# Moving the SBUF pools of a float32 decoder kernel from 64 and 192 bytes past a multiple of 256 onto the multiple itself

## The chip, the cores and the metric

The kernel runs on one core of a Trainium2 chip. The time is the device time of one execution in microseconds (us); the time before is 1786.8 us, the median of three runs (1786.62 to 1786.98). Five engines share the core: TensorE (PE, with its weight loads shown apart as PEld), VectorE (DVE), ScalarE (ACT), GpSimd (POOL) and SyncE (SP, which here only issues DMA). SBUF is the on-chip memory: 128 partitions, each a row of bytes; a tile is a range of bytes at one address in all partitions, and "address" below always means the byte offset in a partition.

## The reference: what is computed

Two residual layers on a sequence of 512 positions with 1024 channels, and a last RMSNorm. All is float32. Per layer:

```
h = rmsnorm(x, norm1_g);  p = h @ w_in                       # 1024 x 7424 columns
y_rw  = rwkv7_branch(...)      # token shift, decay, 8 heads of 64, recurrence over time
y_ret = retention_branch(...)  # rotary, 4 heads, chunks of 128
y_sg  = sgu_branch(...)        # gelu, layer norm, causal mixing in chunks of 128
x = x + sum_g(sigmoid(gate_g) * (y_g @ w_branch[g])) @ w_out
u = rmsnorm(x, norm2_g) @ ffn_w_up                           # 1024 x 5632
c = causal depthwise conv of width 3 over u
x = x + (silu(c[:, :2816]) * c[:, 2816:]) @ ffn_w_down       # 2816 x 1024
```

Nearly all arithmetic is in the products with the large weights.

## The kernel before

**Products in three passes.** A float32 product is made of float32r passes on TensorE. Each operand is split into a rounded part `hi` and a rest `lo` (ScalarE makes `hi` by a cast, VectorE subtracts to get `lo`), and `mm3` (L140) issues three matmuls into one accumulator: weight hi with activation lo, hi with hi, lo with hi. Each is its own pass: a weight load of 128 x 128 (the stationary operand) and a matmul that streams the moving operand, 128 partitions x 512 columns of 4 bytes, that is 2048 contiguous bytes of every partition. `matF` (L152) does this for the k-blocks of one output block of 128 channels. The program has 6,934 such passes with 512 columns and, in `finish` (L945), 132 with 256 columns.

**Weights.** `unit` (L89) gives the next 128 x 512 block of a weight: `load` (L112) issues its DMA from SP into one of three raw buffers `wr`, `part` (L120) makes the hi and lo. The parts lie in the pool `wp` (tiles `wh`, `wl`) in the first half of a layer, and later in the pools of `self.f`, `self.r` or `self.u` (tiles `sh`, `sl`). The order of the units is noted in a first build and replayed in the second with a look-ahead of 2 to 5 units (`AHEAD`, L26).

**Order.** Instructions of one engine run in the order that the tile framework's planner gives; places that must not be moved are pinned (`keep_in_program_order`). In the RWKV-7 part, products of the gates, retention and spatial gating are handed out as filler (`fillers`, L350) between the dependent steps: 33 steps of filler while `solve` (L632) inverts the chunk matrices on VectorE, then one step between the steps of the recurrence (L542 to L611).

**Where tiles lie.** The pools are laid one behind another in every partition, in the order in which they are opened (L55 to L59), and each tile takes its bytes rounded up to 32. A 16 KiB area for DMA and four constants of 32 bytes come first, so `cp` begins at 16,512. With the sizes of the code:

| pool | what it holds | address before | past a multiple of 256 |
|---|---|---|---|
| `cp` | `con` 3748 bytes, `rst` 2048, `bonesR` 512, `ones` 512 | 16,512 | `con` 128, the rest 64 |
| `wp` | `wr`, `wh`, `wl`: 3 tiles of 2048 each | 23,360 | 64 |
| `up` | 31 tiles of 2048 (`self.u`): normed `hi`/`lo`, gate and conv tiles, `x` | 41,792 | 64 |
| `rg` | 16 tiles of 2048 (`self.r`) | 105,280 | 64 |
| `sp` | small tiles: two buffers of each unless said otherwise; `rsF`, the row of norm factors, is one buffer of 528 columns of which 512 are used; `R` | 138,048 | mixed; `rsF` 64, `R` 192 |
| `rw0`, `rw1` (first half of a layer) | `GB`, `F`, `UB`, `ag`, `bk`, `cs`, ... | 145,856 | `GB` 192, `ag`, `bk`, `cs` 64 |
| `ff0`, `ff1` (the rest of the layer) | 39 tiles of 2048 (`self.f`) | 145,856 | 192 |

Tiles of 2048 bytes keep the remainder of their pool, and slices of weights start at multiples of 512 bytes inside a tile, so every operand of `mm3` starts at its pool's remainder.

**Which passes stream from which pool.** From `ff` (192 past): per layer the merges of three branches (L864: 24 x 4 k-blocks x 3 passes = 288), `wout` (L877: 8 x 8 x 3 = 192), the transposed spatial-gating product (L812: 4 x 8 x 3 = 96) and four triples in `rwkv_out` (12); and in `ffn_down` (L924) the tiles `ah`, of which 39 of 44 lie in `ff` (L896 to L898): 59 of 66 passes per output block, 15 blocks, 885. In all 2 x 588 + 885 = 2,061, and 118 of the 132 passes of 256 columns. The other 4,873 passes of 512 columns stream from `up`, `wp` or `rg` (64 past): all of `ffn_up` (L892), the RWKV columns, gates and retention projections.

The functions touched are `norm_rows` (L226, the buffer `rsF`), `run` (L258, the tile `ones`) and `rwkv` (L384, the tile `omu`, 1 minus the token-shift weight, read by `col` at L412).

Of the kernel before, what the change touches and what calls it, by code (L numbers as in the profile page):

```python
# [8 lines left out]
F32 = mybir.dt.float32  # L9
# [37 lines left out]
class Emit:  # L47
# [178 lines left out]
    def norm_rows(self):  # L226
        pb = self.sm()
        for c in range(NC):
            self.tc.keep_in_program_order(self.nc.tensor.transpose(pb[:, c * 128:c * 128 + 128], self.rsT[:, c:c + 1].to_broadcast([128, 128]), self.c("ident")))
        self.rsF = self.small((128, 528), "rsF", bufs=1)[:, :512]  # L230
        self.nc.scalar.copy(self.rsF, pb)

    def firstF(self, l, ids, st, at):
# [24 lines left out]
    def run(self):  # L258
        nc, tc, a, V = self.nc, self.tc, self.a, self.nc.vector
        self.con = self.cp.tile([128, NCC], F32, name="con")  # L260
        self.rst = self.cp.tile([128, 512], F32, name="rst")
        self.bonesR = self.cp.tile([128, 128], F32R, name="bonesR")
        self.ones = self.cp.tile([128, 128], F32, name="ones")
        V.memset(self.rst, 1.0)
        V.memset(self.ones, 1.0)
        nc.scalar.copy(self.small((128, 1), "ms"), self.rst[:, 0:1])
        wu = self.acc()
        for i in range(6):
            nc.tensor.matmul(wu[:, 0:256], self.rst[:, 0:128], self.rst[:, 256:512], start=True, stop=True)
        self.load_pc(0)  # L270
        st = self.norm_new()
        xs = [self.u(n="x") for _ in range(8)]
        self.keep = True
        with tc.high_priority():
            for j in range(8):
                tc.keep_in_program_order((nc.scalar if j in (1, 3) else nc.sync).dma_start(xs[j], a["xT"][:, j, :]))
                if self.plan and j in (0, 2, 3):
                    self.load(self.plan[self.nraw])
        for step in "z0 w z1 z2 w z3 w z4 z5 w z6 z7 w s0 s1 s2 w s3 s4 s5 s6 s7".split():
            if step == "w":  # L280
                if self.plan:
                    if self.nraw == self.npart:
                        self.load(self.plan[self.nraw])
                    self.part(self.plan[self.npart])
            elif step[0] == "z":
                self.norm_z(st, xs[int(step[1])], "n1")
            else:
                self.norm_sq(st, xs[int(step[1])])
        self.keep = False
        tc.keep_in_program_order(nc.scalar.dma_start(self.con, a["con"]))  # L290
        xd = [a["xT"][:, j, :] for j in range(8)]
        for l in range(L):
            mg = self.mixer(l, st)
            st = self.norm_new()
            x = self.wout(l, mg, xd, st)
            act = self.ffn_up(l, st)
            st = self.norm_new()
            x, xd = self.ffn_down(l, act, x, st)
            if l == L - 1:
                self.finish(l, act, x, st["acc"])  # L300
            self.rp.__exit__(None, None, None)
            self.fp = None
# [81 lines left out]
    def rwkv(self, l, nst):  # L384
# [1 line left out]
        T, P = nc.tensor, nc.gpsimd  # L386
        q8 = lambda t: t.rearrange("p (c t) -> p c t", t=64)
        pcol = lambda n, w: self.pc[:, PC[n]:PC[n] + w]
        omu = self.small((128, 14), "omu")
        V.tensor_scalar(omu, pcol("mu", 14), -1.0, 1.0, op0=MUL, op1=ADD)  # L390
        haw = self.small((128, 8), "haw")
        V.tensor_scalar(haw, pcol("a0", 8), 0.5, None, op0=MUL)
# [722 lines left out]
```

## Time and profile before

| | |
|---|---|
| time, median of 3 runs | 1786.8 us |
| the profiled execution | 1787.56 us, its span 1785.5 us |
| granted TensorE clock over the span | 0.997 |
| PE busy | 1770.2 us, 9,646 matmuls |
| VectorE busy | 1160.3 us |
| ScalarE busy | 784.7 us |
| GpSimd busy | 192.9 us |
| bytes moved by DMA | 193.27 MB, 108 GB/s over the span |
| the longest chain | PE 97% of the span, line 144 alone 88% |

The profile names instructions by line: all passes of `mm3` stand at L144, told apart by tile names, written `acc<-moving,stationary`. The mean duration of a matmul there is its time from first to last column through a pipeline; passes overlap, so that what a pass costs is the distance from its start to the next one's start. That is read from the timeline, which lists the start of every instruction.

### The profile page before, as it was taken

How to read it: one execution, taken by the hardware profiler on the slowest of the kernel's cores; microseconds unless marked ns; L12 is line 12 of the kernel's file. 1: busy time of each engine (PE TensorE's matmuls, PEld its weight loads, DVE VectorE, ACT ScalarE, POOL GpSimd, SP SyncE). 2: the span in 40 equal slices, each digit the busy share in tenths (PEclk: the TensorE clock that was granted, in tenths of full speed). 3: DMA queues.
4: the chain of work that ended last, by engine and by line, in shares of the span. 5: the costliest groups of instructions: out<-in, count | busy, mean ns of one | idle time of the engine just before them, and what ended most of it. 6: DMA issues, size and time to landing. Idle time of an engine off the chain costs nothing.

```text
span 1785.5 us, 25916 instructions
## 1 busy us (share of the span) xinstructions
PE 1770.2 (99%) x9646; PEld 1443.6 (81%) x9646; DVE 1160.3 (65%) x1996; ACT 784.7 (44%) x1333; POOL 192.9 (11%) x240
## 2 busy tenths in 40 slices
PE   9999999999999999999999999999999999999998
PEld 7878877888788888888887788778887888888887
DVE  6887736468667777753358875455676687777333
ACT  5564444544344444343245544445332454443321
POOL 0132012013300000000002220220132000000000
PEclk9999999999999999999999999999999999999999
DMA  5234432324543333243332343324144433332332
GB/s 161 80 91 145 134 108 77 108 74 155 166 136 95 98 97 100 67 119 111 104 95 72 117 143 116 100 77 141 55 160 146 147 95 95 98 97 66 106 95 82
DMA packets 104109, 193.27 MB, mean 108 GB/s; under 512 B 11952, under 2 KB 16304, under 8 KB 103984
## 3 DMA queue, kind: packets, MB, share of 16 engines
q1 hardware_dynamic: 89280, 159.42, 29.1%
q10 hardware_dynamic: 10224, 17.52, 2.9%
q0 software_dynamic: 4480, 14.68, 2.6%
q8 instruction: 76, 1.25, 0.3%
q14 instruction: 49, 0.40, 0.1%
HBM read 174.80 MB, written 16.78 MB: 107 GB/s over the span
## 4 chain that ended last, share of the span: by engine, by line
PE 97%; DVE 1%; ACT 1%; issue 1%; DMA 1%; POOL 0%; POOLq 0%; DVEq 0%; ACTq 0%
PE acc L144 88%; PE sm L561 1%; PE sm L486 1%; PE sm L442 1%; PE sm L568 1%; PE sm L577 0%; PE sm L591 0%; PE sm L856 0%; PE sm L453 0%; DMA x<-xT 0%; PE sm L772 0%; PE sm L551 0%; PE sm L761 0%; PE sm L687 0%; PE sm L144 0%
## 5 line engine op out<-in xcount | busy, mean ns | idle before, releaser
L144 PE MATMUL acc<-lo,sh 128*128 128x512 f32 x1056 | 415.4, 394 | 1.0 <-DVE lo L137 0.8
L144 PE MATMUL acc<-hi,sh 128*128 128x512 f32 x1056 | 414.8, 393 | 0.0
L144 PE MATMUL acc<-hi,sl 128*128 128x512 f32 x1056 | 413.2, 392 | 0.0
L127 ACT CAST sh<-wr 128x512 fp32r<-128x512 f32 x376 | 228.2, 611 | 394.6 <-PE acc L144 300.0
L128 DVE TENSOR_TENSOR sl<-wr,sh 128x512 fp32r<-128x512 f32 x376 | 256.1, 685 | 194.2 <-PE acc L144 101.4
L144 PE MATMUL acc<-lo,wh 128*128 128x512 f32 x640 | 253.6, 396 | 1.9 <-DVE lo L203 1.6
L144 PE MATMUL acc<-hi,wh 128*128 128x512 f32 x640 | 250.9, 392 | 0.0
L144 PE MATMUL acc<-hi,wl 128*128 128x512 f32 x640 | 250.2, 392 | 0.0
L144 PEld LDWEIGHTS acc<-lo,sh 128*128 128x128 f32 x1056 | 198.5, 188 | 44.4 <-issue 1.8
L127 ACT CAST wh<-wr 128x512 fp32r<-128x512 f32 x208 | 128.6, 619 | 238.4 <-PE acc L144 223.2
L144 PEld LDWEIGHTS acc<-hi,sl 128*128 128x128 f32 x1056 | 198.5, 188 | 42.3
L144 PEld LDWEIGHTS acc<-hi,sh 128*128 128x128 f32 x1056 | 198.5, 188 | 41.9
L128 DVE TENSOR_TENSOR wl<-wr,wh 128x512 fp32r<-128x512 f32 x208 | 150.6, 724 | 121.6 <-ACT wh L127 118.5
L144 PE MATMUL acc<-ah,sh 128*128 128x512 f32 (+1 forms) x748 | 223.1, 382 | 0.0
L144 PEld LDWEIGHTS acc<-ah,sh 128*128 128x128 f32 x748 | 137.5, 188 | 29.9
L144 PEld LDWEIGHTS acc<-lo,wh 128*128 128x128 f32 x640 | 120.5, 188 | 29.3 <-DVE lo L203 1.9
L144 PE MATMUL acc<-ah,sl 128*128 128x512 f32 (+1 forms) x374 | 142.6, 381 | 0.0
L144 PEld LDWEIGHTS acc<-hi,wl 128*128 128x128 f32 x640 | 120.4, 188 | 27.2 <-issue 1.1
L144 PEld LDWEIGHTS acc<-hi,wh 128*128 128x128 f32 x640 | 120.7, 189 | 25.6 <-issue 1.1
L907 DVE TENSOR_TENSOR fu<-acc,rsF 128x512 f32<-128x512 f32 x88 | 60.7, 690 | 69.3 <-PE acc L144 69.1
L909 ACT ACTIVATE cv<-fu,pc 128x512 f32<-128x512 f32 x88 | 71.9, 817 | 43.9 <-DVE fu L907 39.0
L144 PEld LDWEIGHTS acc<-ah,sl 128*128 128x128 f32 x374 | 70.2, 188 | 14.9
(277 smaller groups left out, 2171.6 us busy)
## 6 DMA issues: line engine op xcount, KB each, us to landing
wr<-wall SPq DMA_DIRECT2D x488, 256.0 KB, 2.6
wr<-wdn SPq DMA_DIRECT2D x80, 256.0 KB, 2.7
gd<-gth ACTq DMA_DIRECT2D x48, 256.0 KB, 3.4
gth<-gd POOLq DMA_DIRECT2D x48, 256.0 KB, 3.4
tab<-rot ACTq DMA_DIRECT2D x8, 256.0 KB, 3.2
xi<-xT SPq DMA_DIRECT2D x8, 256.0 KB, 3.4
wr<-wdn SPq DMA_DIRECT2D x16, 128.0 KB, 2.1
xd<-xi POOLq DMA_DIRECT2D x8, 256.0 KB, 2.7
```

What stands on the lines that cost most here:

```text
L127: self.kept(self.nc.scalar.copy(hi[:, :n], raw[:, :n]))
L128: self.kept(self.nc.vector.tensor_tensor(lo[:, :n], raw[:, :n], hi[:, :n], op=SUB))
L144: i = self.nc.tensor.matmul(*x, **y)
L442: T.matmul(o, w[ks, ms], x[ks, :], start=i == 0, stop=i == 2)
L486: T.matmul(pgs[h][:, j, :], bk[hv[h], c, :, :].rearrange("p a t -> p (a t)"), ag[hv[h], h, c, :], start=True, stop=True)
L561: po(T.matmul(o[hv[h], m, :], AG[m][:, h, c, i:i + 64], w[:, m, h, :], start=m == 0, stop=i == 0, skip_group_check=True))
L568: po(T.matmul(pu[hv[h], 0, m, :], GB[:, 8 * m + c, 0:64], ub[:, m, h, :], start=m == 0, stop=True, skip_group_check=True))
L907: V.tensor_tensor(u, ps, self.rsF, op=MUL)
L909: A.activation(t, u, AF.Identity, scale=self.p("cw2", j), bias=self.p("cb", j))
```

## The change

The change alters the size of three tiles and no instruction. `ones` is allocated with 176 columns instead of 128, of which the first 128 are used as before: 192 bytes more, which moves `wp`, `up`, `rg` and what follows by 192. `omu` gets one buffer instead of two: 64 bytes less. `rsF` gets 512 columns instead of 528: 64 bytes less.

```
-        self.rsF = self.small((128, 528), "rsF", bufs=1)[:, :512]
+        self.rsF = self.small((128, 512), "rsF", bufs=1)
...
-        self.ones = self.cp.tile([128, 128], F32, name="ones")
+        self.ones = self.cp.tile([128, 176], F32, name="ones")[:, 0:128]
...
-        omu = self.small((128, 14), "omu")
+        omu = self.small((128, 14), "omu", bufs=1)
```

By the table of addresses, `wp` then begins at 23,552, `up` at 41,984, `rg` at 105,472 (all multiples of 256), and the pools behind `sp` at 145,856 + 192 - 64 - 64 = 145,920, which is 570 x 256. `R` and `GB` come to a multiple too; `ag`, `bk` and `cs` come to 128 past one and `rsF` to 192 past. `con`, `rst`, `bonesR` and `ones` stay where they are. With one buffer, the `omu` of the second layer waits until the first layer's has been read.

## The prediction

> **What bounds the kernel now.** The page's busy times and its chain come first.
>
> ```profile
> PE 1770.2 (99%) x9646; PEld 1443.6 (81%) x9646; DVE 1160.3 (65%) x1996; ACT 784.7 (44%) x1333; POOL 192.9 (11%) x240
> PE 97%; DVE 1%; ACT 1%; issue 1%; DMA 1%; POOL 0%; POOLq 0%; DVEq 0%; ACTq 0%
> ```
>
> TensorE is busy in 99% of the span and carries 97% of the chain. The view of the waits says how little it stands still for others: nine lines, 8.8 us together, the longest of them these.
>
> ```profile
> PE acc L144 <- DVE lo L203: 1.6, 1, 1.6
> PE sm L807 <- DVE sgg L784: 0.9, 1, 0.9
> PE sm L680 <- DVE cs L666: 0.7, 1, 0.7
> ```
>
> So the time is the number of passes times the distance between their starts. That distance is in the timeline, and this is the view that decides the case. First `ffn_up`, whose moving tiles lie in `up`, 64 past a multiple of 256; then `ffn_down`, whose `ah` lie in `ff`, 192 past (a line with x2 holds two passes); then `finish`, 256 columns, mostly from `ff`.
>
> ```profile
> 599.75 0.39 PE L144 MATMUL acc<-hi,sl 128*128 128x512 f32 x1
> 599.98 0.39 PE L144 MATMUL acc<-lo,sh 128*128 128x512 f32 x1
> ...
> 601.79 0.39 PE L144 MATMUL acc<-hi,sl 128*128 128x512 f32 x1
> ...
> 837.79 0.63 PE L144 MATMUL acc<-ah,sh 128*128 128x512 f32 x2
> 838.26 0.40 PE L144 MATMUL acc<-ah,sl 128*128 128x512 f32 x1
> ...
> 839.90 0.63 PE L144 MATMUL acc<-ah,sh 128*128 128x512 f32 x2
> ...
> 1766.23 0.40 PE L144 MATMUL acc<-ah,sh 128*128 128x256 f32 x2
> ...
> 1767.66 0.40 PE L144 MATMUL acc<-ah,sh 128*128 128x256 f32 x2
> ```
>
> From 599.75 to 601.79 nine passes start, 2.04 / 9 = 226.7 ns each. From 837.79 to 839.90 nine start, 2.11 / 9 = 234; over the longer run 767.93 to 770.03 of the same product it is 2.10 / 9 = 233.3, which I use. The 256-column passes take 1.43 / 12 = 119. The granted clock is 1.00 in both stages, and neither waits for another engine. So the same instruction with the same bytes costs 6.6 ns more from one pool than from the other; what differs in the code is the remainder of the moving address and the place in SBUF. Further, the price isn't proportional to columns: (226.7 - 119) / 256 = 0.42 ns per column gives 215 for 512 columns, and 12 are left over per pass.
>
> The second view is the float32 matmuls that aren't split, by line with shapes kept apart and one of them in the timeline.
>
> ```profile
> L761 PE MATMUL sm<-qB,kF 128*128 128x256 f32 x32 | 8.9, 378 | 0.0
> L848 PE MATMUL sm<-ws,ones 128*128 128x512 f32 x4 | 2.0, 592 | 0.0
> 422.83 1.03 PE L761 MATMUL sm<-qB,kF 128*128 128x256 f32 x4
> ```
>
> Four of them take 1.03 us from first start to last end and the last one 0.378, so (1.03 - 0.378) / 3 = 217 ns lie between starts. The 256 columns more of L848 cost 592 - 378 = 214 ns, 0.836 per column, twice the 0.42 above. At this half rate a pass has 217 - 214 = 3 ns over its columns, although `qB` too starts 64 past; at the full rate it has 12 to 20. The surplus thus appears where the stream is read at full rate. 12 to 13 ns are the time of 30 to 32 columns, 128 bytes: what a stream would lose that touches one more 128-byte piece because its start isn't at the start of one (2048 bytes from 64 past lie in 17 such pieces, from a multiple in 16). That is my reading of the rows, not something a row states.
>
> VectorE and ScalarE show no such price: by line, the subtraction into `ff` takes what one within `up` takes, and so do the casts.
>
> ```profile
> L917 DVE TENSOR_TENSOR fth<-fth,cv 128x512 f32<-128x512 f32 x44 | 30.1, 685 | 0.3
> L920 DVE TENSOR_TENSOR ah<-fth,ah 128x512 fp32r<-128x512 f32 x44 | 30.0, 683 | 4.2 <-ACT ah L919 4.2
> ```
>
> **The change part by part.** Nothing is removed or added on any engine or queue. Three edits move addresses.
>
> `omu` with one buffer: the second layer's write (L390, VectorE, 174 ns, at 775.2 us) must wait for the last reads of the first layer's. Those are the scaled copies of L412 in the RWKV columns, which the order puts ahead of the first `solve`, ended at 205 us; the wait is 570 us past due and costs nothing. Without that distance every VectorE instruction behind L390 would stand, and TensorE behind them.
>
> `rsF`: same reads, other remainder; VectorE rows don't depend on it: nothing.
>
> Moved pools: the passes. No pass of 512 columns starts at a multiple of 256 in this trace, so I bound its distance. From below: the columns alone, 214 (from L848) to 215. From above: the 226.7 of the better remainder; that it could be worse still is a rival. The nearest row is the half-rate pass, with 512 column-times in 217 ns, in which a surplus of reading would be hidden: I take 216, a little under, as its 1.03 is rounded.
>
> - From 64: 4,873 passes, less about 70 before 27 us, which ran at a lower granted clock or waited for the input: 4,803 x (226.7 - 216) = 51.4 us.
> - From 192: 2,061 x (233.3 - 216) = 35.7 us.
> - The 256-column passes: 132 x 8 = 1.0 us (119 to 111; between 0 and 1.5).
> - Some 2,580 short float32 passes: their starts are mostly 64 or 192 past now; they run at half rate or are bounded by weight loads: 0, at most 1 ns each either way.
>
> Gross: 88.1 us. Here two rules of the Trainium skill can be held against the rows. The page "TensorE: Matmul & The Clock Gate" (section "Wait — 56ns, not 53.3ns?") puts back-to-back 512-column matmuls 215.7 ns apart at full clock, whatever the address; the trace has 226.7 and 233.3, so something not in that rule is paid here, and were it all gone, an estimate by that page would come out 2 us below mine. The page "SBUF — State Buffer" (section "Specifications (TRN2)") gives lines of 16 bytes; 64, 192 and 256 are all multiples of 16, and by that rule the sum would be zero.
>
> What comes back: TensorE faster means that others are late. In the second layer's `solve`, VectorE's last transpose that the matmuls need ends when TensorE arrives (the 0.7 us wait at L680); the 255 filler passes ahead of it gain 2.7 us that is lost there. In the first layer that transpose ends at 203.5 and TensorE arrives at 207.7, more slack than the 2.9 us gained. The rest by the stages:
>
> ```profile
> 175.00:207.00 32.00, 32.00 (x143) 26.50 (x142) 29.50 (x60) 11.48 (x18) 1.36 (x2) 1.00 0.41 130
> 545.00:767.00 222.00, 222.00 (x981) 183.86 (x980) 173.98 (x269) 104.61 (x163) 0.00 (x0) 1.00 0.29 90
> 1060.00:1090.00 30.00, 29.30 (x140) 24.01 (x139) 27.11 (x60) 10.02 (x16) 0.00 (x0) 1.00 0.46 144
> ```
>
> Columns: length, then busy time of PE, PEld, DVE, ACT, POOL, granted clock, DMA share, GB/s. VectorE is at 78% in `ffn_up` and would be at 174 / 211.5 = 82%; in the two `solve` stretches it is at 90 to 92% and nearly full afterwards. A weight block then has 12 x 216 = 2.59 us instead of 2.72, against 2.6 us from issue to landing with three raw buffers in flight: hidden. I add 3 us for waits that grow: 6 us given back in all. At worst none of the gain in 20 to 207 and 890 to 1090 us gets through, some 1,400 passes of 512 columns there x 10.7 = 15 us.
>
> Sum: 88.1 - 6 = 82.1. Against the profiled execution, 1787.56 - 82.1 = 1705.5; the median of the runs is 0.76 below that execution, so **1705 us**. Its own ends: 215 to 214 and nothing given back, 4,803 x 12.7 + 2,061 x 19.3 + 1.5 = 102.3, with 2 us for the short passes: 1683. And 217 with 15 given back: 81 - 15 = 66: 1721.
>
> **The rivals.**
>
> *Half way.* If only part of the surplus is the start (the rest the swap of weights, say), at 221 ns: 4,803 x 5.7 + 2,061 x 12.3 = 52.7, less 4: 1738. For it: nothing in the rows separates the 12 ns.
>
> *A fixed price.* The 12 ns belong to every full-rate pass and only 192 past is bad: all at 226.7, 2,061 x 6.6 = 13.6 us, 1773. For it: 226.7 is very steady. Against: the half-rate passes, with a weight load each too, have 3 ns.
>
> *Nothing changes.* The 6.6 ns come from where `ff` lies or from its stage, and multiples of 64 bytes are enough: 1787. The 16-byte lines of the Trainium skill's page "SBUF — State Buffer" would come to the same. Against: two stages with the same engines idle or busy, and only one price per pool.
>
> *Slower.* The order in which the weight load and the stream reach the same piece of SBUF decides: both are 64 past in the good case, 64 and 192 in the bad one; starting both at 0 could make them collide in every pass as in the bad case. All at 233.3: 4,803 x 6.6 = 31.7 us more, 1818. It decides from a distance of (4,803 x 226.7 + 2,061 x 233.3) / 6,864 = 228.7 on. Against: both start at the same remainder today in `ffn_up`, and that is the good case.
>
> **How the numbers follow.** A measurement of this kernel tells 0.2% (3.6 us) from no change. Chances: 0.73 for the forecast, 0.09 half way, 0.08 fixed price, 0.04 nothing, 0.06 slower. Faster is the sum of the first three, 0.90. The range from 1683 to 1745 takes in the forecast's own ends and half way; the other 0.18 lie outside.
>
> **What would show it.** `ffn_up` and `ffn_down` at the same distance, 214 to 217, nine starts in 1.94 us; TensorE's waits up from 8.8 to 12 to 18 us, first at L680 in the second layer; VectorE and ScalarE rows unchanged within 1%. Wrong it is if `ffn_up` stays at 226.7, or rises, or if TensorE's starts come closer and its waits grow by tens of us.

## The result, and the profile after

The changed kernel takes 1775.6 us (median of four runs, 1774.56 to 1778.42) against 1786.7 us: ratio 0.9941, 95% interval 0.9924 to 0.9958. It is faster, by 0.6%, and far outside the range given (1683 to 1745); the rival called "a fixed price" had 1773. The profiled execution took 1774.56 us, 13.0 less than that of before; the medians differ by 11.1.

The busy times of the changed kernel, from its page:

```profile
PE 1756.1 (99%) x9646; PEld 1442.5 (81%) x9646; DVE 1161.7 (66%) x1996; ACT 784.8 (44%) x1333; POOL 192.6 (11%) x240
```

TensorE loses 14 us of busy time; the others stay. The instructions of every engine stand in the same order as before, but for two neighbours on VectorE near 7 us (L505 and a weight split of L128). In the timeline of the changed kernel, the three places that the prediction showed (`ffn_up`, `ffn_down`, `finish`; start, length, what):

```profile
599.18 0.39 PE L144 MATMUL acc<-lo,sh 128*128 128x512 f32 x1
...
601.22 0.39 PE L144 MATMUL acc<-lo,sh 128*128 128x512 f32 x1
...
837.86 0.62 PE L144 MATMUL acc<-ah,sh 128*128 128x512 f32 x2
...
839.90 0.62 PE L144 MATMUL acc<-ah,sh 128*128 128x512 f32 x2
...
1752.31 0.40 PE L144 MATMUL acc<-ah,sh 128*128 128x256 f32 x2
...
1753.75 0.40 PE L144 MATMUL acc<-ah,sh 128*128 128x256 f32 x2
```

`ffn_up`: nine passes in 2.04 us, 226.7 ns, exactly as before. `ffn_down`: nine in 2.04 us, 226.7 where it was 233.3. `finish`: twelve in 1.44, 120 where it was 119, although 118 of its 132 passes stream from `ff`. So the passes of 512 columns from `ff` came down to the price of all others, and that price did not move. The groups by line with shapes apart say the same: 660 passes at 395 ns became 390, here after.

```profile
L144 PE MATMUL acc<-ah,sh 128*128 128x512 f32 x660 | 203.3, 390 | 0.0
```

Summed over the passes in their order, the distances between starts are 11.6 us shorter for the passes from `ff` and 1.5 us for the other float32r passes. Of this 1.5, 1.2 come within the first hundred passes, and say little of addresses: from 10 to 14 us the profile of before has a granted clock of 0.57 (passes start 427 ns apart there), that of after 1.00. This can be why the two profiled executions differ by more than the medians. The waits of TensorE in the changed kernel, the three longest and the one that the prediction named:

```profile
PE acc L144 <- DVE rst L505: 1.6, 1, 1.6
PE acc L269 <- DVE rst L264: 1.5, 1, 1.5
PE acc L144 <- DVE lo L203: 1.5, 2, 1.2
...
PE sm L680 <- DVE cs L666: 0.7, 1, 0.7
```

The nine lines add up to 10.3 us, against 8.8.

### The profile page after: what moved, and what is told of

Read it like the earlier page. It is cut to its first block, busy times and chain, and to the rows that moved or that the text cites. A ratio compares the mean times of both kernels' runs of the same rounds, so it can differ in the third digit from the quotient of the medians.

```text
span 1772.5 us, 25916 instructions
## 1 busy us (share of the span) xinstructions
PE 1756.1 (99%) x9646; PEld 1442.5 (81%) x9646; DVE 1161.7 (66%) x1996; ACT 784.8 (44%) x1333; POOL 192.6 (11%) x240
## 4 chain that ended last, share of the span: by engine, by line
PE 97%; issue 1%; ACT 1%; DVE 1%; DMA 0%; POOLq 0%; POOL 0%; DVEq 0%
PE acc L144 89%; PE sm L561 1%; PE sm L486 1%; PE sm L442 1%; PE sm L568 1%; PE sm L577 0%; PE sm L591 0%; PE sm L856 0%; PE sm L772 0%; PE sm L761 0%; PE sm L453 0%; DMA x<-xT 0%; PE sm L551 0%; PE sm L687 0%; PE sm L144 0%
## 5 line engine op out<-in xcount | busy, mean ns | idle before, releaser
L128 DVE TENSOR_TENSOR sl<-wr,sh 128x512 fp32r<-128x512 f32 x376 | 257.5, 689 | 183.4 <-PE acc L144 99.4
L128 DVE TENSOR_TENSOR wl<-wr,wh 128x512 fp32r<-128x512 f32 x208 | 150.7, 725 | 121.7 <-ACT wh L127 118.5
```

The costliest lines, as they stand in the source:

```text
L128: self.kept(self.nc.vector.tensor_tensor(lo[:, :n], raw[:, :n], hi[:, :n], op=SUB))
```

## The experiments

After the result, two questions were open. Why does a tile of `ff` cost 6.6 ns more when it is 192 past and nothing more at 0, if 64 and 0 cost the same elsewhere? And what are the 12 to 13 ns over the columns, which stayed? For the first there were three theories: the moving remainder itself (A), the difference between the moving tile's and the weights' remainder (D; in the kernel before, weights were 64 past, so `ff` stood 128 from them and nearly everything else 0), or the place in SBUF or the stage (P).

### The bare streams

A kernel of its own, with no other engine at work: 48 float32r passes per section, weights (eight slices of `wr`) and moving tile (three slices of `xr`) at chosen remainders. Its core (`NP` is 48; `...` marks what is left out):

```
        for name, t, ow, om, n, k, change in RUN:
            w, m, size = tiles[t]
            ...
            for i in range(NP):
                sw = (i % 8 if change else 0) * 128 + ow // size
                sx = (i // 2 % 3 if n == 512 else 0) * 512 + om // size
                tc.keep_in_program_order(nc.tensor.matmul(
                    p[:k, :n], w[:, sw:sw + k], m[:, sx:sx + n], start=i == 0, stop=i == NP - 1))
```

> This kernel leaves out the whole computation: it streams 48 passes per section from tiles at chosen remainders (w = weights, m = moving tile, bytes past a multiple of 256), with no other engine at work. Three theories for the 6.6 ns that ff tiles cost: (A) the moving remainder 192 itself is dear: every section with m192 at about 233 ns between starts, whatever w, all with m0 or m64 at 227. (D) the difference of the two remainders counts: w0m0, w64m64, w128m128 and w192m192 all at 227, sections with a difference of 128 (w0m128, w64m192, w192m64) at 233. (P) neither, it is the place in SBUF or the stage: all sections at 227. For the 13 ns over the columns that are left everywhere: (S) a fixed price per float32r pass: sections with fewer columns all lie 13 ns over 0.417 ns per column, and 96, 64 or 32 weight columns change nothing; (W) it is the weight load: fewer weight columns make it smaller in proportion, to 10, 7 and 3 ns; (R) it is the reading of 4 bytes per column: bfloat16 passes of 512 columns lie at 214 to 217.

Its timeline has one line per section (name w, m: remainder of weights and moving tile); the distance is the start of the next section less the start of this one, over 48.

```profile
24.51 11.17 PE L63 MATMUL w0m64x<-xr,wr 128*128 128x512 f32 x48
35.52 11.32 PE L63 MATMUL w0m128x<-xr,wr 128*128 128x512 f32 x48
46.67 11.36 PE L63 MATMUL w0m192x<-xr,wr 128*128 128x512 f32 x48
57.87 11.36 PE L63 MATMUL w64m0x<-xr,wr 128*128 128x512 f32 x48
69.07 11.06 PE L63 MATMUL w64m64x<-xr,wr 128*128 128x512 f32 x48
79.97 11.17 PE L63 MATMUL w64m128x<-xr,wr 128*128 128x512 f32 x48
90.97 11.32 PE L63 MATMUL w64m192x<-xr,wr 128*128 128x512 f32 x48
102.13 11.31 PE L63 MATMUL w128m0x<-xr,wr 128*128 128x512 f32 x48
...
290.81 10.07 PE L63 MATMUL cols448x<-xr,wr 128*128 128x448 f32 x48
300.71 8.49 PE L63 MATMUL cols384x<-xr,wr 128*128 128x384 f32 x48
...
316.07 5.92 PE L63 MATMUL cols256x<-xr,wr 128*128 128x256 f32 x48
321.83 5.50 PE L63 MATMUL cols192x<-xr,wr 128*128 128x192 f32 x48
...
332.50 11.23 PE L63 MATMUL load96x<-xr,wr 128*96 128x512 f32 x48
343.56 11.21 PE L63 MATMUL load64x<-xr,wr 128*64 128x512 f32 x48
354.61 11.29 PE L63 MATMUL load32x<-xr,wr 128*32 128x512 f32 x48
365.74 11.08 PE L63 MATMUL samew_x<-xr,wr 128*128 128x512 f32 x48
376.66 10.53 PE L63 MATMUL bfl_x<-xb,wb 128*128 128x512 bf16 x48
387.03 10.52 PE L63 MATMUL bfm_x<-xb,wb 128*128 128x512 bf16 x48
```

`w0m64` takes 11.01 / 48 = 229.4 ns, `w0m128` 232.3, `w0m192` 233.3, `w64m0` 233.3, `w64m64` 227.1. Moving tiles 192 past cost 233.3 with weights at 0 and 232.5 with weights at 64; a moving tile at 0 costs 233.3 with weights at 64. All sixteen pairs, in ns:

| weights \ moving | 0 | 64 | 128 | 192 |
|---|---|---|---|---|
| 0 | 226.7 | 229.4 | 232.3 | 233.3 |
| 64 | 233.3 | 227.1 | 229.2 | 232.5 |
| 128 | 232.3 | 233.5 | 227.5 | 229.4 |
| 192 | 229.2 | 232.3 | 233.3 | 227.5 |

(0, 0 ran first, and eleven of its passes started 427 ns apart; its 226.7 is from the second such kernel, below.) Each diagonal, moving less weights, has one price: 0 about 227, 64 about 229, 128 about 232, 192 about 233. That is D alone; A would have made a column dear and P nothing. D had named only the difference of 128 as dear; that 192 is dearer was new.

On the second question: 256 columns take 5.76 / 48 = 120, so 107 ns less than 512: 12 to 13 remain over the columns (fixed, S). At 320 and 384 columns 13 remain too, but 448 columns take 9.90 / 48 = 206, which leaves 19, and 192 and 128 columns both take 111, where S had 93 and 66: S holds in part only. Fewer weight columns don't help, 230.4, 230.2 and 231.9 for 96, 64 and 32 (W falls). bfloat16 passes take 10.37 / 48 = 216, at either remainder (R holds so far: it goes with four bytes per column).

### All pools 192 past

```
-        self.ones = self.cp.tile([128, 128], F32, name="ones")
+        self.ones = self.cp.tile([128, 160], F32, name="ones")[:, 0:128]
-        self.rsF = self.small((128, 528), "rsF", bufs=1)[:, :512]
+        self.rsF = self.small((128, 560), "rsF", bufs=1)[:, :512]
```

> The kernel before with all large pools 192 past a multiple of 256 (ones 160 columns, rsF 560). Theory A (a moving tile 192 past is dear): 6,864 passes at 233.3, 31.7 us over the kernel before, 1818 us. Theory D (the difference to the weights' remainder counts): no difference anywhere, all at 227, 1774 to 1777 us, as the changed kernel. Theory P (place or stage): 1786 us.

1775.5 us (1775.0 to 1776.6), ratio to the kernel before (1785.8 us beside it) 0.9941 (0.9929 to 0.9954). In the groups by line of this kernel, the 660 passes stand as in the changed one:

```profile
L144 PE MATMUL acc<-ah,sh 128*128 128x512 f32 x660 | 203.3, 389 | 0.0
```

The whole gain with every large pool at the remainder that was dear before: A is out by 42 us.

### All pools 64 past

Of the kernel before, `rsF` alone:

```
-        self.rsF = self.small((128, 528), "rsF", bufs=1)[:, :512]
+        self.rsF = self.small((128, 560), "rsF", bufs=1)[:, :512]
```

> The kernel before with ff moved from 192 to 64 past a multiple of 256 (rsF 560 columns), so that all large pools are 64 past one. Theories A and D: 1774 to 1777 us, the whole gain without a multiple of 256 anywhere. If the multiple of 256 itself matters: 1780 us or more. Theory P: 1786 us.

1774.6 us (1773.5 to 1776.4), ratio 0.9935 (0.9921 to 0.9948). What lies behind `rsF` in `sp`, and with it `rw0`, `rw1` and `ff`, moved by 128 bytes and nothing else: that is the whole gain, and the multiple of 256 has no part in it. Of what moved, `ff` holds the tiles whose passes became shorter.

### The changed kernel with ff 128 past

```
-        self.rsF = self.small((128, 512), "rsF", bufs=1)
+        self.rsF = self.small((128, 544), "rsF", bufs=1)[:, :512]
```

> The changed kernel with ff alone moved to 128 past a multiple of 256 (rsF 544 columns). Theory D: the passes whose moving tile lies in ff and whose weights lie at a multiple go from 226.7 to 233 ns, 2,061 x 6.6 = 13.6 us, 1786 to 1789 us. Theory A (192 alone is dear): 1774 to 1777 us.

1785.2 us (1784.6 to 1787.7), ratio 0.9998 (0.9990 to 1.0007): the gain is gone, with all pools but one at a multiple of 256 and `ff` at another remainder than before, but at the same difference of 128. The time is a little under the 1786 to 1789 that D had. In its groups:

```profile
L144 PE MATMUL acc<-ah,sh 128*128 128x512 f32 x660 | 207.1, 395 | 0.0
```

### The stream pool drawn away from the weights

Two gaps, so that `up` starts at a multiple of 256 while `wp` and `rg`, where the weights lie, stay 64 past one:

```
         self.wp = tp("wp", 2)
+        tp("gap1", 1).tile([128, 48], F32, name="gap1")
         self.up = tp("up", NU)
+        tp("gap2", 1).tile([128, 16], F32, name="gap2")
         self.rg = tp("rg", NR)
```

> The kernel before with two gaps between pools: up starts at a multiple of 256, wp and rg stay 64 and ff 192 past one. Theory D (the difference of moving minus weights remainder counts; prices from the bare streams: 0 gives 227, 64 gives 229.3, 128 gives 232.3, 192 gives 233.3 ns): some 4,130 passes with weights in wp or rg and a moving tile in up go from difference 0 to 192, 27.2 us, and the 576 of the two-sided retention products from 0 to 64, 1.5 us: 1813 to 1816 us. Theory A (the moving remainder counts) and the reading of the prediction (a multiple of 256 streams cheapest): 1786 us or less.

1812.1 us (1811.4 to 1813.5) against 1786.1, ratio 1.0149 (1.0132 to 1.0166): slower, although the tiles streamed most now start at a multiple. 26 us instead of the 27 to 30 expected; the size is a little off, the direction not, and A and the prediction's reading had nothing or a gain. In its timeline (lines are numbered two higher) `ffn_up` has what `ffn_down` had:

```profile
599.15 0.39 PE L146 MATMUL acc<-hi,sl 128*128 128x512 f32 x1
...
601.25 0.39 PE L146 MATMUL acc<-hi,sl 128*128 128x512 f32 x1
```

Nine passes in 2.10 us, 233.3.

### Finer differences, and where the rest comes from

The bare streams again, with alternating remainders, differences below 64 bytes, fixed addresses, and operands read from one address (a broadcast view):

```
sw = w[:r, c:c + 1].to_broadcast([r, 128]) if "zw" in d else w[:r, c:c + 128]
sx = x[:r, c:c + 1].to_broadcast([r, 512]) if "zm" in d else x[:r, c:c + 512]
```

> This kernel too leaves out the whole computation and streams 48 passes per section. Which weights count: altown alternates passes of remainders (0, 0) and (128, 128), altnext (0, 128) and (128, 0). If a stream meets the load of its own weights, altown is at 227 and altnext at 232; if it meets the load of the next pass's weights, the other way round. Finer differences: if the price follows the 64-byte steps, 4 to 12 bytes cost nothing and 244 to 252 too; if it begins with the first byte, 4 is already over 230. far: differences of whole multiples of 256 at fixed addresses, 227 each if nothing beyond 256 bytes counts. The 11 ns between a float32r pass (227) and a bfloat16 pass (216): if they come from reading weights and stream at once, onew (all weight columns from one address) or onem (all moving columns from one address) is at 216; if the float32r pass simply lasts longer, both stay at 227. Fewer rows (64, 32): 227 if it is a matter of columns.

```profile
24.78 11.04 PE L66 MATMUL base_x<-xr,wr 128*128 128x512 f32 x48
35.66 11.14 PE L66 MATMUL altown_x<-xr,wr 128*128 128x512 f32 x48
46.63 11.20 PE L66 MATMUL altnext_x<-xr,wr 128*128 128x512 f32 x48
57.67 11.56 PE L66 MATMUL w0m4x<-xr,wr 128*128 128x512 f32 x48
69.07 11.37 PE L66 MATMUL w0m8x<-xr,wr 128*128 128x512 f32 x48
...
213.40 11.26 PE L66 MATMUL onew_x<-xr,wr 128*128 128x512 f32 x48
224.50 10.65 PE L66 MATMUL onem_x<-xr,wr 128*128 128x512 f32 x48
235.08 11.19 PE L66 MATMUL rows64x<-xr,wr 64*128 64x512 f32 x48
```

`altown` takes 228.5, `altnext` 230.0: neither 227 nor 232, so this pair of sections doesn't say which weights a stream meets. Four bytes of difference cost 237.5 already, more than any step of 64. The other small differences with weights at 0, by the same reckoning: 8 bytes 233.5, 12 bytes 228.8, 208 bytes 235, 232 bytes 234, 244 bytes 239.4, 248 bytes 234, 252 bytes 229.0; and of the first such kernel, 16 bytes 231.7, 32 bytes 233.3, 240 bytes 226.9. So the price begins with the first bytes, as the second guess had it, but it is not even.

The same kernel has two more sections with a difference of 240 bytes, at other remainders:

```profile
147.49 11.36 PE L66 MATMUL w16m0x<-xr,wr 128*128 128x512 f32 x48
158.69 11.35 PE L66 MATMUL w128m112x<-xr,wr 128*128 128x512 f32 x48
169.88 11.04 PE L66 MATMUL far0x<-xr,wr 128*128 128x512 f32 x48
```

They take 233.3 and 233.1, where weights at 0 and a moving tile at 240 took 226.9. So below steps of 64 bytes the difference alone does not set the price; the difference rule is shown for the sixteen pairs of multiples of 64 alone. Differences of 256, 512 and 1024 at fixed addresses cost nothing (226.7 each). All weight columns from one address: 231; all moving columns from one address: 10.58 / 48 = 220 including the change of section, 218.7 between starts inside it. So most of the 11 ns lie in reading the stream. With 64 rows a pass takes 227 ns once the section has settled (231 to 236 at first), as with 128; the section with 32 rows ran at a granted clock near 0.58 and says nothing.

### Which part of the reading

> Streams alone again, nothing of the reference is computed. turn: five passes with weights from wr (difference 0), then one from ws (difference 128). If a stream meets the load of its own weights, the pass with ws is the long one (232); if it meets the load of the next pass's weights, it is the pass ahead of it; if the price is a matter of the pair in turn, it is spread. For the 11 ns between float32r (227) and bfloat16 (216): one address for all moving columns took it to 218.7. again N: the stream repeats its first N columns: if what costs is distinct reads of SBUF pieces, it falls with N at the size of the piece (64 columns are 256 bytes, 16 are 64); if it is only the fixed address, every again N from 4 on is at 227. each N: every column N times in a row, so that new bytes are wanted at a half, a quarter, an eighth of the rate: 216 to 219 if the rate of reading costs, 227 if the pass itself lasts longer. step: every second column, twice the bytes crossed: 227 if bytes used count, far more if bytes crossed count. bothone: 216 to 219.

The edit is the view of the moving tile: `again N` repeats the first N columns, `each N` gives every column N times, `step` takes every second column; `turn` has weights from a second tile `ws`, 128 past, in every sixth pass.

```profile
23.87 11.04 PE L74 MATMUL base_x<-xr,wr 128*128 128x512 f32 x48
34.75 1.30 PE L74 MATMUL turn_x<-xr,wr 128*128 128x512 f32 x5
35.89 0.40 PE L74 MATMUL turn_x<-xr,ws 128*128 128x512 f32 x1
36.12 1.30 PE L74 MATMUL turn_x<-xr,wr 128*128 128x512 f32 x5
...
66.73 10.66 PE L74 MATMUL again4x<-xr,wr 128*128 128x512 f32 x48
77.22 11.79 PE L74 MATMUL again16x<-xr,wr 128*128 128x512 f32 x48
88.85 11.53 PE L74 MATMUL again32x<-xr,wr 128*128 128x512 f32 x48
100.22 11.08 PE L74 MATMUL again64x<-xr,wr 128*128 128x512 f32 x48
...
132.90 10.52 PE L74 MATMUL each2x<-xr,wr 128*128 128x512 f32 x48
143.25 10.52 PE L74 MATMUL each4x<-xr,wr 128*128 128x512 f32 x48
...
163.97 21.96 PE L74 MATMUL step_x<-xr,wr 128*128 128x512 f32 x48
185.76 11.08 PE L74 MATMUL end_x<-xr,wr 128*128 128x512 f32 x48
```

- `turn`: six passes take 1.37 us, 13 to 14 ns more than six at 226.7. By the single starts, the pass ahead of the one with `ws` lasts 233 and the one with `ws` 234, the rest 226 to 227. One foreign pass makes two dear: the one ahead of it, and its own. Both single answers expected fall; the third holds. But by this every pass of `altown` and `altnext` would be dear, and they took 228.5 and 230.0: how mixed passes add up is not shown.
- `each 2`, `each 4` and `each 8` take 10.35 / 48 = 216, as bfloat16: a float32r pass isn't longer in itself; wanting new bytes at half the rate takes the 11 ns away. `step`, twice the bytes crossed, takes 21.79 / 48 = 454, twice 227: bytes crossed count.
- `again 64` (256 bytes round and round) takes 227, `again 32` 237, `again 16` 242, `again 4` (one piece of 16 bytes) 218.6, as `again 1` and `bothone`. Streams that turned back after 64 and 128 bytes paid more, those that stayed within 16 less. That was not expected: the price didn't fall with N.

## Why the prediction was wrong

**The bound.** Right. The time is passes times distance, and nothing else came to bind: the average distance of undisturbed float32r passes of 512 columns went from 229.0 to 227.3 ns, and 1.7 ns x 6,934 passes is 11.8 us, the change of the time (11.1) within 1 us.

**The two prices.** Right as read, 226.7 for `ffn_up` and 233.3 for `ffn_down`, and right that the address makes the 6.6. But 233.3 was not the price of all passes from `ff`: from 490 to 520 us, among the merges and `wout`, the passes started 232.4 ns apart on average before and 226.7 after. Wrong in what of the address: not the moving tile's remainder, but its difference to the weights'. The trace of before held both remainders with one and the same weights' remainder, and couldn't tell. The prediction came nearest in the rival that it gave 0.06, which made the weight load's and the stream's meeting decide; what spoke against it there, that `ffn_up` had both at one remainder and was the good case, was the answer.

**The step that failed** is the value taken for the distance at a multiple of 256, 216, with the reading under it that the 12 to 13 ns are a piece of 128 bytes touched because of the start. Measured: 226.7, at 0 as at 64 (`ffn_up` after, the diagonal of the table). The 51.4 us of the passes from 64 were thus nothing: 1.5 us in the trace, 1.2 of it among the first passes, where the granted clock of the two profiles differs. The 35.7 us of the passes from 192 were 2,061 x 6.6 = 13.6 by this distance, 11.6 by the sum over the trace, since not every pass from `ff` had stood at 233.3. Among them 24 in `rwkv_out` have their weights in `ff` too, so a difference of 0 before and after; they did not get shorter (about 231 ns both times, where they did not wait). The 1.0 us of `finish` was nothing, 119 to 120. The surplus of the full-rate stream is real and I had its condition (full rate) right: at half the rate it goes, in bfloat16 and in `each 2`. Its cause I had wrong, and nothing in the rows pointed at the start of the moving tile; a reading that fitted two numbers was used as if it were a price.

**The page's 215.7.** The section of "TensorE: Matmul & The Clock Gate" of the Trainium skill that I set beside the rows holds here for bfloat16 (216) and for float32r streams that want new bytes at half the rate (216), and not for the passes of this kernel. The same page of the Trainium skill says (section "Step-by-step: what each phase is for") that loading the next weights doesn't steal read bandwidth from the running matmul; the table of sixteen pairs doesn't fit this, since the weights' address alone changes the distance by up to 6.6 ns. By the 16-byte lines of the Trainium skill's page "SBUF — State Buffer" (section "Specifications (TRN2)"), as the prediction used them, the sixteen pairs would be equal; they are not.

**What comes back.** The 6 us given back belonged to a gain that didn't come; TensorE's waits rose by 1.5 us, and the one at L680, named as the first to grow, stayed at 0.7, since the filler passes ahead of it got no shorter. `omu` cost nothing (L390 still 174 ns, no wait for the first layer's reads), and the VectorE and ScalarE rows stayed, as said.

**The rivals.** That the kernel got faster at all, as forecast, was luck by the prediction's own reasoning: the edit put streams and weights at one remainder, which any common remainder would have done. "A fixed price" had the time, 1773 against 1775.6, with the wrong reason for 192. "Nothing changes" is refuted by the result and by the run with all pools 64 past, "slower" by the result; but the run with `up` drawn away shows that an address change of the same kind can cost 26 us.

**What stays open.** Whether reads collide and which, why the price of a difference isn't even (4 bytes 237.5, 12 bytes 228.8, 64 bytes 229, 192 bytes 233), and why 240 bytes cost nothing at one pair of remainders and 6.5 ns at two others. Also why passes of 256 columns have no such price: in `finish` they start 119 ns apart at a difference of 128 (the kernel before, and `ff` 128 past), 117.5 at 192 (`up` drawn away) and 120 at 0. That the price belongs to the pair of weights and stream is shown by the table and by `turn`; that the two reads share something is the likely reading, and what they share, no run shows. Of the 11 ns at difference 0, the runs show that they go with reading the stream at full rate, not why it is 13 over the columns for 256 and 512 alike. No version beat the changed kernel clear of the noise: the three with difference 0 throughout (0, 64 and 192 past) lie within 0.1% of each other.

## What to carry to other kernels

In a kernel whose time is float32r passes of 512 columns, let the tiles that are streamed and the tiles that are loaded as weights have the same remainder past a multiple of 256 bytes; which remainder was of no account at 0, 32, 64, 128 and 192. A pad of 128 bytes in a small tile ahead of a pool was worth 0.6%, and pads of 192 and 64 bytes around the wrong pool cost 1.5%. And a price that the trace shows at two addresses bounds nothing at a third: where the nearest row differs in kind (here the rate of the stream), the end that the same kind of pass shows deserves the larger chance.

## What was not expected of the hardware

- The start of a pass's moving tile has no price of its own: 226.7 to 227.5 ns at 0, 32, 64, 128 and 192 past a multiple of 256 as long as the weights have the same remainder (32 with 32: 227).
- Differences of 64, 128 and 192 bytes cost 2.5, 5.5 and 6.6 ns a pass of 512 columns; 4 and 244 bytes cost 11 and 13; 240 bytes cost nothing with weights at 0 and 6.5 with weights at 16 or 128.
- Passes of 256 columns did not pay for a difference: 119 ns at 128 bytes, 120 at 0.
- One pass whose weights stand apart makes its neighbour dear as well: 233 and 234 among passes of 226.7.
- A float32r stream that gives each column twice runs at 216 ns, one that turns back every 16 columns at 242.
